# Low parts of split weights by an accumulating DMA instead of subtractions, in a two-layer decoder step

## The chip, the cores and the metric

The kernel runs on one core of a Trainium2 chip. The metric is the device time of one execution in microseconds (us), as the median over runs. A core has TensorE (PE: matmuls; its weight loads are listed apart as PEld), VectorE (DVE), ScalarE (ACT), GpSimd (POOL), SyncE (SP: here it issues most DMAs) and sixteen DMA engines that move data between HBM and the on-chip SBUF. Matmul results go to PSUM, which TensorE fills and VectorE and ScalarE empty.

## The reference

One inference step of two layers over 520 rows (512 prompt rows and 8 sample rows) of 1024 channels, in float32:

```
layer 0:  z = x @ w_in                     # 1024 -> 7 * 1024
          a_val, a_gate, b_post, c_pre, h, g = split(z)
          a = silu(layer_norm(causal_conv31(a_val * sigmoid(a_gate))))
          s = causal_conv3(c_pre * h)
          x = layer_norm(alpha * x + (concat(a, b_post * s) * silu(g)) @ w_out)
layer 1:  u, v, g = split(x @ w_in)        # 1024 -> 3 * 2048
          u, v = gelu(u), layer_norm(gelu(v))
          mix = tril(w_s) @ v + b          # in chunks of 128 rows, 8 heads
          x = layer_norm(alpha * x + (u * mix * silu(g)) @ w_out)
```

The step also returns the convolutions' new caches and the sample rows' v. Both convolutions run per channel.

## The kernel before

Channels lie on the 128 partitions and rows along the free axis, so that x is eight tiles of 128 x 520. All weights are cut into 136 *units* of 128 output channels by 1024 inputs ([128, 8, 128], 512 KB). The products keep float32 accuracy with TensorE's float32r type in three matmuls each: a weight unit is split into `hi` (its float32r rounding) and `lo` (what is left), x likewise, and a product is hi x hi + lo x hi + hi x lo. A unit over all 520 rows is 48 matmuls (8 k tiles, 2 halves of 260 rows, 3 terms) in `mm2` (L152, matmul at L157); `mm` does one half in 24 (L141).

Units 0 and 1 are loaded and split tile by tile together with x at the start (from L179, products at L207, tiles `w0h`, `w0l`). The 134 others come through `load_unit` (L116): SyncE loads `raw` (L119, three buffers), ScalarE casts it to `whi` (L121), and VectorE or GpSimd subtracts to get `wlo` (L124). GpSimd has the units of `ON_POOL`, 4 to 45 and 66 to 83, VectorE the other 74. `whi` and `wlo` take two of twelve slots, so six units are held; four units that are used while others are loaded take slots of their own. `unit(n)` (L132) calls `load_unit` up to `LEAD` = 5 units ahead of the product that asks for unit n.

The order of each engine's queue is fixed when the kernel is built: a scheduler simulates the program and places each instruction by its simulated time and priority. The taps of the wide convolution have the lowest priority and so fill what VectorE has left. At run time every queue is in order and waits for semaphores.

In layer 0 each i of eight needs four units: gate, value, c and h (z_gate, z_val, z_c, z_h). ScalarE takes the sigmoid `sg` of the gate (L291) and copies c (L317), VectorE makes `apad` (L306) and `ch` (L325), GpSimd copies the sample rows and sends the caches out (L307, L308, L326, L327). The wide convolution is 30 multiply-adds per tile on VectorE (L269) into `acc` in PSUM; the short one two (L332) into `sB` in SBUF, with `ch` in SBUF as well. Then z_post (VectorE multiplies it into `sB`, L392), the gates, and the two parts of the output projection with the layer norm (`out_part`: L487 to L562, its shift matmul at L497). The products `z` have two PSUM buffers; a third and a fourth, in which the products of unit 1 also lie, belong to the convolution. Layer 1 runs v in 16 units, scales it on VectorE (L658), and then takes u, gate and output in groups of four; `mix_unit` copies its sample rows on GpSimd (L725).

Of the kernel before, what the change touches and what calls it, by code (L numbers as in the profile page):

```python
# [9 lines left out]
F32 = mybir.dt.float32  # L10
# [3 lines left out]
ALU = mybir.AluOpType  # L14
# [3 lines left out]
D = 1024  # L18
# [14 lines left out]

# columns of the packed per-channel parameters
PA_W = 0
# [15 lines left out]
def decoder_kernel(  # L51
# [19 lines left out]
    nc = tc.nc  # L71
# [39 lines left out]

# [1 line left out]
    n_units = 2 + wu.shape[0]  # L113
    units = [None, None]

    def load_unit(wtag=("W", 12)):  # L116
        n = len(units)
        raw = wpool.tile([P, KT, P], F32, tag="raw", name=f"raw_{n}", bufs=3)
        nc.sync.dma_start(raw, wu[n - 2])  # L119
        hi = wpool.tile([P, KT, P], F32R, tag=wtag[0], name=f"whi_{n}", bufs=wtag[1])  # L120
        nc.scalar.copy(hi, raw)  # L121
        lo = wpool.tile([P, KT, P], F32R, tag=wtag[0], name=f"wlo_{n}", bufs=wtag[1])
        eng = nc.gpsimd if n in ON_POOL else nc.vector
        eng.tensor_tensor(lo, raw, hi.bitcast(F32), op=ALU.subtract)  # L124
        units.append((hi, lo))

    ON_POOL = set(range(4, 46)) | set(range(66, 84))
    EXTRA = set()
# [35 lines left out]

    # products of a constant until the first rows are there, so that the array's clock is up by then
    warm = const.tile([P, P], BF16, name="warm")
# [4 lines left out]

    # the input rows come with the first two weight units, one k tile after the other, and the
    # products follow in that order
    xh, xl = [], []
# [4 lines left out]
    for k in range(KT):  # L179
        x = tmp(f"x_{k}")  # L180
        if k % 4 == 0:
            raw = wpool.tile([P, 4, 2, P], F32, tag="raw", name=f"raw_s{k}", bufs=3)
# [4 lines left out]
        cuts = 2 if k == 0 else 1  # L187
# [29 lines left out]
    nc.sync.dma_start(pa, pa_in)  # L217
    # powers of two, so float32r holds them as well
    ones_r = const.tile([P, P], F32R, name="ones_r")
# [10 lines left out]

    # ================= layer 0 =================
    unit(1)
# [49 lines left out]
    n = 0  # L282
# [57 lines left out]

    # the sample rows of both convolutions
    nc.gpsimd.dma_start(cbs_out, xb)
# [27 lines left out]

    # layer norm of the wide convolution over the channels, then silu
    def mean_of(m, src, name):
        """the sum of src / D over the channels, from its two float32r parts"""
        both = tpool.tile([P, T], F32R, tag="B", name=f"parts_{name}", bufs=4)
        nn = src.shape[-1]
        hi, lo = both[:, :nn], both[:, TH : TH + nn]
        nc.scalar.copy(hi, src)
        nc.vector.tensor_tensor(lo, src, hi.bitcast(F32), op=ALU.subtract)
        nc.tensor.matmul(m, ones_r, hi, start=True, stop=False)
        nc.tensor.matmul(m, ones_r, lo, start=False, stop=True)  # L380
# [13 lines left out]
    def split_y(i, g, other, tag, parts):  # L394
        """y = g * other as its two parts, in that many cuts of the rows"""
        h = y_slot(F32R, f"yh_{tag}{i}")
        lo = y_slot(F32R, f"yl_{tag}{i}")
        for j in range(parts):
            c = slice(j * T // parts, (j + 1) * T // parts)
            nc.vector.tensor_tensor(g[:, c], g[:, c], other[:, c], op=ALU.mult)  # L400
            nc.scalar.copy(h[:, c], g[:, c])
            nc.vector.tensor_tensor(lo[:, c], g[:, c], h[:, c].bitcast(F32), op=ALU.subtract)
        yh.append(h)
        yl.append(lo)
# [68 lines left out]
    def out_part(base, c0, c1, yh, yl, res, lnc, done, last=False, pool_sub=()):  # L473
        """The second half of an output projection for the rows c0..c1, the residual, and the layer
        norm over the channels. The sums of the norm are of the rows less the mean of their first
        512 channels, so that no large mean cancels in the variance."""
        c = slice(c0, c1)
# [107 lines left out]

    # ================= layer 1 =================
    wt = wpool.tile([P, NH, P], F32, tag="M", name="wt", bufs=4)
    nc.gpsimd.dma_start(wt, wsT_in)
    bs = wpool.tile([P, NH, P], F32, tag="M", name="bs", bufs=4)
    nc.gpsimd.dma_start(bs, bs_in)  # L590
    # wt[s, h, t] is kept where s <= t
    nc.gpsimd.affine_select(
        wt, wt, pattern=[[0, NH], [1, P]], compare_op=ALU.is_ge, fill=0.0, base=0, channel_multiplier=-1
    )
    # and its float32r parts, for the column sums
    wth, wtl = [], []
# [31 lines left out]
    for i in range(NVF):  # L628
        z = one(i, f"z_v{i}_1")[:, :TH]
        mm(z, unit(n + i), x1h, x1l, hs(1))  # L630
        t = vt[i]
# [18 lines left out]
    def v_finish():  # L650
# [5 lines left out]
        for i in range(NV):  # L656
            for c in range(NC):
# [7 lines left out]
                )  # L665
        # column sums of the causal weights, for the shift of the norm
        for j in range(2):
# [5 lines left out]
            )  # L673
        # the sample rows' layer norm
        ssum = tiny.tile([P, NS], F32, name="ssum")
# [113 lines left out]
def _units(w, e0, e1):  # L789
    """[1024, e] columns e0..e1 as [n, 128 (k inside), 8 (k tile), 128]"""  # L790
    w = w[:, e0:e1]
    n = (e1 - e0) // P
    return w.reshape(KT, P, n, P).transpose(2, 1, 0, 3)


def _chan(a, n):
    """[..., n*128] -> [128, n, ...]"""
    a = a.reshape(a.shape[:-1] + (n, P))
    k = a.ndim
    return a.transpose((k - 1, k - 2) + tuple(range(k - 2)))  # L800
# [86 lines left out]
```

## Time and profile before

| | |
|---|---|
| time, median of 3 runs | 842.21 us (840.75 to 844.86) |
| profiled execution | span 840.8 us; its own time is not listed apart, the fastest run is 840.75 |
| granted TensorE clock, mean | 0.991 |
| busy, share of the span | PE 97%, DVE 66%, ACT 37%, POOL 23% |
| DMA | 82.38 MB, mean 98 GB/s; the sixteen engines' packets took 31.2% of the span |
| weight loads (L119) | 134 of 512 KB, median 3.6 us from issue to landing |

A row of the groups of instructions reads: line, engine, operation, out<-in, shapes, count | busy us, mean ns of one | idle time of its engine just before, and what ended it. A row of the stretches reads: from:to, its length, then busy us (and instructions) of PE, PEld, DVE, ACT and POOL, the granted clock of TensorE, the mean busy share of the DMA engines, and GB/s. A row of the timeline reads: start, us, engine, line, operation, count [idle before <- what ended it]. An engine that is not the bottleneck may idle at no cost.

### The profile page before, as it was taken

The page shows a single profiled execution, that of the slowest core. Times are in us where ns is not written, and L with a number is a line of the kernel's source. Part 1 is how long each engine was busy: PE and PEld are TensorE (multiplying, and loading weights), DVE is VectorE, ACT ScalarE, POOL GpSimd, SP SyncE. Part 2 cuts the span into 40 slices and gives each one's busy share as a digit, 9 for nine tenths or more (in the row PEclk, how much of TensorE's full clock was granted, in tenths as well). Part 3 has the DMA queues.
Part 4 walks back from the last instruction along what each step waited for, and adds up shares of the span by engine and source line. Part 5 has one row for each costly group of instructions (what it writes and reads, how often), then busy time and mean ns, then how long its engine had stood idle before and what let it go on. Part 6 is the DMA issues. An engine that isn't in the chain of part 4 may idle for free.

```text
span 840.8 us, 15982 instructions
## 1 busy us (share of the span) xinstructions
PE 816.4 (97%) x6792; PEld 813.8 (97%) x6792; DVE 557.8 (66%) x894; ACT 309.5 (37%) x470; POOL 193.7 (23%) x178
## 2 busy tenths in 40 slices
PE   9989999998999999999999999999999999999994
PEld 8989999998999999999999999999999999999993
DVE  5899999999994487356696333495455433625566
ACT  5423322333124346333466533333432133333243
POOL 0844355544340000024252711101000000000022
PEclk9999999999999999999999999999999999999998
DMA  8533333223223452424050522204223233222011
GB/s 301 164 103 101 101 103 102 96 82 130 72 79 101 122 166 66 126 76 126 26 166 12 171 81 82 95 24 156 77 76 95 82 101 94 83 79 99 1 51 51
DMA packets 27110, 82.38 MB, mean 98 GB/s; under 512 B 3568, under 2 KB 7296, under 8 KB 27040
## 3 DMA queue, kind: packets, MB, share of 16 engines
q1 hardware_dynamic: 26000, 79.01, 30.1%
q0 software_dynamic: 1040, 2.36, 0.7%
q8 instruction: 53, 0.87, 0.4%
q14 instruction: 17, 0.14, 0.1%
HBM read 77.91 MB, written 3.44 MB: 97 GB/s over the span
## 4 chain that ended last, share of the span: by engine, by line
PE 71%; DVE 23%; DMA 2%; issue 2%; ACT 1%; SPq 0%; POOL 0%; ACTq 0%; DVEq 0%; POOLq 0%
DVE acc L269 14%; PE z_gc L157 11%; PE z_u L157 11%; PE z_p L141 9%; PE z_v L157 7%; PE z_q L157 5%; PE z_o L157 5%; PE z_gb L157 5%; PE z_ga L157 5%; PE z_post L157 4%; PE z_v L141 4%; DVE sB L332 3%; DMA raw<-in_wu 2%; PE mix L713 2%; PE vt L615 1%
## 5 line engine op out<-in xcount | busy, mean ns | idle before, releaser
L121 ACT CAST whi<-raw 128x1024 fp32r<-128x1024 f32 x134 | 140.0, 1047 | 300.6 <-issue 66.6
L124 POOL TENSOR_TENSOR wlo<-raw,whi 128x1024 fp32r<-128x1024 f32 x60 | 145.6, 2434 | 262.6 <-ACT whi L121 262.3
L124 DVE TENSOR_TENSOR wlo<-raw,whi 128x1024 fp32r<-128x1024 f32 x74 | 90.2, 1222 | 131.0 <-ACT whi L121 131.0
L269 DVE SCALAR_TENSOR_TENSOR acc<-apad,pa,acc 128x512 f32<-128x512 f32 x240 | 166.6, 748 | 2.5 <-ACT acc L266 0.8
L157 PE MATMUL z_gc<-x1h,whi 128*128 128x260 f32 x256 | 72.9, 285 | 0.0
L157 PE MATMUL z_u<-x1h,whi 128*128 128x260 f32 x256 | 72.4, 283 | 0.0
L157 PE MATMUL z_gc<-x1h,wlo 128*128 128x260 f32 x256 | 72.0, 281 | 0.0
L157 PE MATMUL z_u<-x1l,whi 128*128 128x260 f32 x256 | 72.0, 281 | 0.0
L157 PE MATMUL z_gc<-x1l,whi 128*128 128x260 f32 x256 | 72.0, 281 | 0.0
L157 PE MATMUL z_u<-x1h,wlo 128*128 128x260 f32 x256 | 72.0, 281 | 0.0
L157 PEld LDWEIGHTS z_u<-x1h,wlo 128*128 128x128 f32 x256 | 48.1, 188 | 0.1
L157 PEld LDWEIGHTS z_gc<-x1h,wlo 128*128 128x128 f32 x256 | 48.2, 188 | 0.0
L157 PEld LDWEIGHTS z_u<-x1h,whi 128*128 128x128 f32 x256 | 48.1, 188 | 0.1
L157 PEld LDWEIGHTS z_gc<-x1l,whi 128*128 128x128 f32 x256 | 48.1, 188 | 0.0
L157 PEld LDWEIGHTS z_u<-x1l,whi 128*128 128x128 f32 x256 | 48.1, 188 | 0.0
L157 PEld LDWEIGHTS z_gc<-x1h,whi 128*128 128x128 f32 x256 | 48.1, 188 | 0.0
L725 POOL COPY mix<-mixs 128x8 f32<-128x8 f32 x16 | 3.5, 226 | 186.5 <-DVE gu L752 174.1
L157 PE MATMUL z_v<-x1h,whi 128*128 128x260 f32 x160 | 46.0, 287 | 0.0
L157 PE MATMUL z_v<-x1h,wlo 128*128 128x260 f32 x160 | 45.0, 281 | 0.0
L157 PE MATMUL z_v<-x1l,whi 128*128 128x260 f32 x160 | 44.9, 281 | 0.0
L157 PE MATMUL z_post<-xh,whi 128*128 128x260 f32 x128 | 36.8, 288 | 4.2 <-DVE sB L392 4.2
L157 PE MATMUL z_h<-xh,whi 128*128 128x260 f32 x128 | 36.9, 288 | 4.0 <-DVE apad L306 4.0
(259 smaller groups left out, 2758.5 us busy)
## 6 DMA issues: line engine op xcount, KB each, us to landing
raw<-in_wu SPq DMA_DIRECT2D x134, 512.0 KB, 3.6
xr<-in_xT SPq DMA_DIRECT2D x8, 260.0 KB, 4.6
x<-in_xT SPq DMA_DIRECT2D x7, 260.0 KB, 4.4
out_y<-r SPq DMA_DIRECT2D x8, 130.0 KB, 1.8
out_y<-out SPq DMA_DIRECT2D x4, 260.0 KB, 2.2
raw_s<-in_w SPq DMA_DIRECT2D x8, 128.0 KB, 4.2
xs<-in_cache_a SPq DMA_DIRECT2D x2, 496.0 KB, 9.2
out_cas<-xs POOLq DMA_DIRECT2D x2, 496.0 KB, 4.5
```

The lines of the kernel that those rows point to most:

```text
L121: nc.scalar.copy(hi, raw)
L124: eng.tensor_tensor(lo, raw, hi.bitcast(F32), op=ALU.subtract)
L141: nc.tensor.matmul(ps, a[:, k, :], b[k][:, c], start=(k == 0 and j == 0), stop=(k == KT - 1 and j == 2),)
L157: nc.tensor.matmul(z[h][:, :TH], a[:, k, :], b[k][:, hs(h)], start=(k == 0 and j == 0), stop=(k == KT - 1 and j == 2),)
L269: nc.vector.scalar_tensor_tensor(acc[i], apads[i][:, j : j + SEQ], pa[:, i, PA_W + j : PA_W + j + 1], acc[i], op0=ALU.mult, op1=ALU.add,)
L332: nc.vector.scalar_tensor_tensor(s[:, :SEQ], ch[:, j : j + SEQ], pa[:, i, PB_W + j : PB_W + j + 1], s[:, :SEQ], op0=ALU.mult, op1=ALU.add,)
L615: nc.tensor.transpose(m[:, c * P : (c + 1) * P], vt[i][:, c * P : (c + 1) * P], ident)
L713: nc.tensor.matmul(m[:, c * P : (c + 1) * P], vtok[i][:, c * P : (c + 1) * P], wt[:, h, :], start=True, stop=True)
L725: nc.gpsimd.tensor_copy(t[:, SEQ:], mixs[:, i, :])
```

## The change

Instead of subtracting, ScalarE writes the negated rounding of the unit, -hi, into `wlo` (L124), and a DMA issued on GpSimd reads the unit from HBM a second time and adds it onto `wlo` in SBUF (L125), which leaves w - hi. All 134 units of `load_unit` are done so; the table `ON_POOL` goes. Units 0 and 1, x and every other split stay as they were. (The diff also empties comments; these lines are left out.)

```diff
         hi = wpool.tile([P, KT, P], F32R, tag=wtag[0], name=f"whi_{n}", bufs=wtag[1])
         nc.scalar.copy(hi, raw)
         lo = wpool.tile([P, KT, P], F32R, tag=wtag[0], name=f"wlo_{n}", bufs=wtag[1])
-        eng = nc.gpsimd if n in ON_POOL else nc.vector
-        eng.tensor_tensor(lo, raw, hi.bitcast(F32), op=ALU.subtract)
+
+        nc.scalar.mul(lo, raw, -1.0)
+        nc.gpsimd.dma_start(lo, wu[n - 2], accum_op=ALU.add)
         units.append((hi, lo))
 
-    ON_POOL = set(range(4, 46)) | set(range(66, 84))
     EXTRA = set()
```

ScalarE's queue at the start, where units 2 and 3 (`whi_292` and its neighbour) are split while the first products still run, before:

```order
L200 CAST xh_272<-x_269 128x520
L121 CAST whi_292<-raw_290 128x1024
L121 CAST whi_313<-raw_311 128x1024
L291 ACT_TABLE_LOAD
L291 ACTIVATE sg_345<-z_first 128x520
L266 ACTIVATE acc_593<-apad_347,pa 128x512
```

and now:

```order
L200 CAST xh_272<-x_269 128x520
L121 CAST whi_292<-raw_290 128x1024
L124 ACTIVATE wlo_294<-raw_290 128x1024
L121 CAST whi_314<-raw_312 128x1024
L124 ACTIVATE wlo_316<-raw_312 128x1024
L291 ACT_TABLE_LOAD
L291 ACTIVATE sg_350<-z_first 128x520
L266 ACTIVATE acc_602<-apad_352,pa 128x512
```

Each cast is followed by the negation of the same unit, and two of these now stand ahead of the first sigmoid `sg`.

TensorE's queue where the first products (`z_first`) end and unit 2 is used for the first time (`z_c`), before:

```order
L207 MATMUL z_first_112<-xl_273,whi_s_205 128x260
L157 MATMUL z_c_354<-xh_120,whi_292 128x260
L157 MATMUL z_c_354<-xh_120,wlo_294 128x260
L157 MATMUL z_c_354<-xl_121,whi_292 128x260
L157 MATMUL z_c_354<-xh_120,whi_292 128x260
```

and now:

```order
L207 MATMUL z_first_112<-xl_273,whi_s_205 128x260
L157 MATMUL z_c_359<-xh_120,whi_292 128x260
L157 MATMUL z_h_417<-xh_120,whi_314 128x260
L157 MATMUL z_c_359<-xh_120,wlo_294 128x260
L157 MATMUL z_c_359<-xl_121,whi_292 128x260
```

One product of unit 3 (`z_h`), whose PSUM buffer is that of `z_first`, has come ahead of the first that uses unit 2's low part.

GpSimd's queue from the first convolution tile on, before:

```order
L307 COPY xs_335<-apad_347 128x8
L308 DMA out_cap<-apad_347 128x30
L124 TENSOR_TENSOR wlo_321<-raw_317,whi_319 128x1024
L124 TENSOR_TENSOR wlo_327<-raw_323,whi_325 128x1024
L124 TENSOR_TENSOR wlo_333<-raw_329,whi_331 128x1024
L124 TENSOR_TENSOR wlo_359<-raw_355,whi_357 128x1024
L326 COPY xb<-ch_466 128x8
L327 DMA out_cbp<-ch_466 128x2
```

and now:

```order
L125 DMA wlo_294<-in_wu 128x1024
L125 DMA wlo_316<-in_wu 128x1024
L307 COPY xs_340<-apad_352 128x8
L308 DMA out_cap<-apad_352 128x30
L125 DMA wlo_323<-in_wu 128x1024
L125 DMA wlo_330<-in_wu 128x1024
L125 DMA wlo_337<-in_wu 128x1024
L125 DMA wlo_364<-in_wu 128x1024
L125 DMA wlo_422<-in_wu 128x1024
L326 COPY xb<-ch_473 128x8
L327 DMA out_cbp<-ch_473 128x2
```

Every subtraction there has become the issue of a transfer, and units 2 and 3, which VectorE had, stand in this queue as well.

## The prediction

> **What bounds the kernel now.** The page's first part, then the waits of TensorE, then the groups of instructions.
>
> ```profile
> PE 816.4 (97%) x6792; PEld 813.8 (97%) x6792; DVE 557.8 (66%) x894; ACT 309.5 (37%) x470; POOL 193.7 (23%) x178
> ```
>
> TensorE is busy 816.4 of 840.8 us, so the 24 us around its matmuls are all that the change can win. Part of that is the start and the end of the program; the rest stands in the waits of TensorE (who waited for whom: us in total, times, longest).
>
> ```profile
> PE z_post L157 <- DVE sB L392: 4.2, 1, 4.2
> PE z_h L157 <- DVE apad L306: 4.0, 1, 4.0
> PE shift L497 <- DVE tot L492: 0.8, 1, 0.8
> PE z_c L157 <- DVE wlo L124: 0.2, 1, 0.2
> ```
>
> Two stalls of 4 us, both on VectorE. What made VectorE late before the one at 47 to 51 us is in the timelines of VectorE and GpSimd (start, us, instruction):
>
> ```profile
> 33.42 2.38 DVE L332 SCALAR_TENSOR_TENSOR sB<-ch,pa,sB 128x512 f32<-128x512 f32 x1 [0.91 <-ACT sB L330]
> 36.37 7.68 DVE L332 SCALAR_TENSOR_TENSOR sB<-ch,pa,sB 128x512 f32<-128x512 f32 x1
> 50.16 0.69 DVE L306 TENSOR_TENSOR apad<-z_val,sg 128x520 f32<-128x520 f32 x1
> ...
> 36.37 7.13 POOL L124 TENSOR_TENSOR wlo<-raw,whi 128x1024 fp32r<-128x1024 f32 x3
> ```
>
> One multiply-add of VectorE took 7.68 us and ended just after three subtractions of GpSimd that began with it (36.37 + 7.13 = 43.50). It reads two operands in SBUF. The wide convolution's steps, whose accumulator is in PSUM, never did this:
>
> ```profile
> L269 DVE SCALAR_TENSOR_TENSOR acc<-apad,pa,acc x240: 737/747/757, 23.4 to 247.5; 128x512 f32<-128x512 f32 x120
> L332 DVE SCALAR_TENSOR_TENSOR sB<-ch,pa,sB x16: 739/1154/7678, 33.4 to 207.1; 128x512 f32<-128x512 f32 x16
> L332 DVE SCALAR_TENSOR_TENSOR sB<-ch,pa,sB 128x512 f32<-128x512 f32 x16 | 29.3, 1831 | 0.9 <-ACT sB L330 0.9
> L358 DVE TENSOR_TENSOR proda<-xs,pa 128x992 f32<-128x992 f32 x2 | 6.5, 3273 | 0.0
> 160.00:200.00 40.00, 40.00 (x338) 40.00 (x338) 39.93 (x55) 11.31 (x15) 18.11 (x14) 1.00 0.32 106
> ```
>
> L332 runs in 739 ns alone and in 1831 ns on average: 16 x 1.09 = 17.5 us lost beside GpSimd. L358 (992 columns) should take about the 1.22 us of a VectorE subtraction of 1024 columns (L124 below): 2 x 2.05 = 4.1 us. So about 21 us of a VectorE that is full (39.93 of 40 us in the last row, third figure) go to waiting for GpSimd before 211 us.
>
> **The change part by part.** It removes the subtractions and adds a ScalarE pass and a second load per unit.
>
> ```profile
> L121 ACT CAST whi<-raw 128x1024 fp32r<-128x1024 f32 x134 | 140.0, 1047 | 300.6 <-issue 66.6
> L124 POOL TENSOR_TENSOR wlo<-raw,whi 128x1024 fp32r<-128x1024 f32 x60 | 145.6, 2434 | 262.6 <-ACT whi L121 262.3
> L124 DVE TENSOR_TENSOR wlo<-raw,whi 128x1024 fp32r<-128x1024 f32 x74 | 90.2, 1222 | 131.0 <-ACT whi L121 131.0
> L308 POOL DMA_DIRECT2D out_cap<-apad x8 | 4.7, 583 | 0.1
> ```
>
> Busy time: GpSimd loses 145.6 us and gains 134 issues of about 0.58 us (78 us); VectorE loses 90.2 us; ScalarE gains 134 x 1.05 = 140 us, to 450 of 841. None of these is on TensorE's path by itself. Behind each added ScalarE pass wait the evacuations of PSUM; two PSUM buffers give them one unit of TensorE's time, 5.7 us (row below), against 2.1 us for a cast and its negation: nothing, unless ScalarE is already late.
>
> *Won: the two stalls.* With no GpSimd arithmetic on weights VectorE is 21 us earlier by 211 us. It was 4.2 us too late there; closing the first stall brings TensorE's demands 5.6 us forward, and 21 covers both. After a stall the array is also slow for a while:
>
> ```profile
> 50.90:55.00 4.10, 4.09 (x21) 4.09 (x22) 4.07 (x7) 2.14 (x3) 4.06 (x4) 0.58 0.02 4
> 211.90:215.10 3.20, 3.12 (x15) 3.12 (x16) 3.20 (x4) 0.00 (x0) 1.82 (x1) 0.53 0.05 17
> 478.88 5.73 PE z_v L157 x48
> ```
>
> The granted clock was 0.58 and 0.53 in these stretches: 21 matmuls in 4.10 us where 5.73/48 = 0.119 us each gives 34, and 15 for 27: 1.6 and 1.4 us. Won: 4.0 + 1.6 + 4.2 + 1.4 = 11.2, and the 0.8 of the shift, where L561 was drawn out in the same way beside GpSimd. 12.0 us; bounds 12.0 and 0 (if VectorE's order and not GpSimd makes it late).
>
> *Lost: the start.* Unit 2, the first that comes through the changed code, is needed the moment the first products end:
>
> ```profile
> 17.71 0.28 PE L157 MATMUL z_c<-xh,whi 128*128 128x260 f32 x1
> 18.20 0.39 PE L157 MATMUL z_c<-xh,wlo 128*128 128x260 f32 x1 [0.20 <-DVE wlo L124]
> 15.84 1.05 ACT L121 CAST whi<-raw 128x1024 fp32r<-128x1024 f32 x1 [0.83 <-DMA raw<-in_wu]
> 18.80 1.05 ACT L121 CAST whi<-raw 128x1024 fp32r<-128x1024 f32 x1 [1.91 <-DMA raw<-in_wu]
> 19.86 1.28 ACT L291 ACT_TABLE_LOAD   x1
> 21.16 0.60 ACT L291 ACTIVATE sg<-z_first 128x520 f32<-128x520 f32 x1
> ```
>
> Its cast ends at 16.9, the negation at 17.95; only then does the accumulating transfer start, with the DMA engines full:
>
> ```profile
> 10.00:20.00 10.00, 9.80 (x82) 9.59 (x82) 5.95 (x11) 5.74 (x11) 0.00 (x0) 1.00 1.02 367
> raw<-in_wu SPq DMA_DIRECT2D x3, 512.0 KB, 5.9
> xs<-in_cache_a SPq DMA_DIRECT2D x2, 496.0 KB, 9.2
> out_cas<-xs POOLq DMA_DIRECT2D x2, 496.0 KB, 4.5
> ```
>
> No row shows an accumulating transfer. From 14 to 25 us a plain 512 KB took 5.9 us from issue to landing; an accumulate also reads its destination, one more pass of 0.524 MB / 367 GB/s = 1.43 us: 7.3 us, landing at 25.3, 7.1 us after 18.2. I take this value, since it is the row of the same size and place. From below: the new order puts a z_h product before the first low part, and that waits for the sigmoid to free its PSUM buffer, which ScalarE reaches at 18.80 + 2 x 1.05 + 1.28 + 0.60 = 22.8: 4.6 us at least. From above: 9.2 + 1.4 after 17.95 is 28.6, 10.4 us. With 1.5 us of slow clock: 8.6 us (6.1 to 11.9). The next units, one per 5.73 us, have their transfers issued by 21.5 and about 27 and are not late.
>
> The Trainium skill, "DMA: Bandwidth & Descriptors", section Anatomy of one DMA, fits 2.0 us plus bytes over 436 GB/s for a DMA issued on GpSimd, 3.2 us here; the row of 4.5 us above is already longer. By it the transfer lands near 21.2, the sigmoid decides, and the sum ends at its lower bound. That is a rival below.
>
> *Steady state.* A unit's slots come free five units, 28.7 us, before it is needed; casts 2.1, issue 0.6 and a landing even as at the start, 7.3, make 10. Hidden, if the DMA engines keep up: plain load 1.43 us of all sixteen engines, accumulate with two reads 2.86, together 4.29 of TensorE's 5.73 per unit. The bounds of the accumulate are 1.43 (the second read costs nothing) and no known top; the point where it decides is 4.30 us, three plain passes.
>
> In GpSimd's queue an accumulate now stands behind small copies that wait for others; the longest such waits are these:
>
> ```profile
> L612 POOL COPY vs<-v 128x8 f32<-128x8 f32 x16 | 8.5, 538 | 51.7 <-ACT v L641 51.7
> L725 POOL COPY mix<-mixs 128x8 f32<-128x8 f32 x16 | 3.5, 226 | 186.5 <-DVE gu L752 174.1
> ```
>
> Each waits for something that the program makes once per unit, so what is queued behind it (an accumulate, and TensorE five units later) loses at most one unit, 5.7 us: 15.7 of the 28.7. At the layers' boundary, where units are freed every 24 matmuls (2.9 us) instead of 48, eight units are freed before the first is used, and eight times 4.29 us of DMA fits into the 23 us of that pass plus the 17 of the next. Both cost nothing, and the full price of a lost cover would be a unit's stall, 5.7 + 1.5 us, at each place.
>
> One place eats most of the cover. VectorE scales v in one block of 16.5 us:
>
> ```profile
> 546.84 16.52 DVE L658 TENSOR_SCALAR vtok<-vtok,mv,rs 128x128 f32<-128x128 f32 x64 [0.41 <-POOL rs L655]
> ```
>
> If GpSimd cannot issue beside it, 16.5 + 10 = 26.5 of the 28.7 us are used; with a pile of two transfers behind it (2 x 2.86) 3.5 us are missing. I put 0 into the sum, since L308 was issued in 583 ns beside a VectorE that was full, and keep the case as rival D.
>
> The Trainium skill, "SBUF — State Buffer", section Two separate sides, speaks against the change here: a VectorE instruction in a two-port mode locks GpSimd out of the port through which it writes DMA descriptors. No GpSimd transfer runs beside L658 in this trace, so it shows neither.
>
> **Sum.** 840.8 - 12.0 + 8.6 = 837.4 us for the profiled execution. Its span is 840.8, the fastest run 840.75, the median 842.2, 1.4 above: 838.8 for the median, with the forecast's own range 836 to 842.
>
> **The rivals.**
> *A. The DMA engines become the bound (slower).* In the steady state, from 4.30 us per accumulate. For it: nothing here prices the addition, and the reads of weights double. Against: 4.29 of 5.73 with two reads. At three and a half passes a unit takes 6.44 us and 134 units 863; at four, 7.15 and 958. Each further pass adds 192 us.
> *B. The start is hidden further.* The landing is short and the sigmoid decides: 842.2 - 12.0 + 6.1 = 836.3. For it: POOL-issued transfers elsewhere took 4.5 us. Against: DMA share 1.02.
> *C. VectorE stays late.* The stalls come from the written order of its queue: 842.2 + 8.6 = 850.8. For it: VectorE is full even without the waiting. Against: 7.68 us beside 7.13.
> *D. The block of VectorE at 547 us holds GpSimd's transfers back.* 3.5 us missing and 1.5 of slow clock: 838.8 + 5.0 = 843.8. For it: the cover is down to 2.2 us there. Against: nothing like it beside the convolution.
>
> **How the numbers follow.** Forecast 0.48, B 0.22, A 0.18, C 0.07, D 0.05. A measurement of this kernel can tell about 0.5%, 4.2 us, from no change: faster is below 838.0, slower above 846.4. Of the forecast (836 to 842, centred on 838.8) a third is faster, 0.16, and 0.03 goes to a start that costs more than its bound, slower. Of B 0.20 is faster. Faster 0.16 + 0.20 = 0.36; slower A 0.18 + C 0.07 + 0.03 = 0.28; within 0.29 + 0.02 + D 0.05 = 0.36. The range reaches below to B with 2 us for stalls that I count as staying, 834, and above over C to where A begins, 858; what it leaves out is most of A, 0.17.
>
> **What would show it.** The waits of TensorE: no z_h on apad, no z_post on sB; a new one of z_c (or z_h) on the transfer or the sigmoid, 5 to 10 us, before 30 us. L332 back to 0.74 us each. DMA share near 0.75. Wrong, if TensorE waits for wlo all along (A), or if the two old stalls stand (C).

## The result and the profile after

The changed kernel takes 847.34 us in the median (846.28 to 848.2), the kernel before 842.21 (840.75 to 844.86): a ratio of 1.0055, with a 95% interval of 1.0039 to 1.0072. It is 0.55% slower where the forecast was 838.8 us, 0.4% faster. The profiled executions have spans of 845.0 and 840.8 us, so the 4.2 us can be followed in the traces, and what has to be explained is 845.0 against the 837.4 of the prediction's sum: 7.6 us.

The page of the changed kernel has these rows: the busy time of each engine with its share of the span, then the DMA queues with packets, MB and the share of the sixteen engines' span that their packets took. The software queue had 2.36 MB in the kernel before; the 134 accumulates bring it to 72.62.

```profile
PE 817.8 (97%) x6792; PEld 814.2 (96%) x6792; DVE 431.2 (51%) x820; ACT 433.6 (51%) x604; POOL 159.1 (19%) x252
...
q0 software_dynamic: 20336, 72.62, 46.3%
q1 hardware_dynamic: 26000, 79.01, 33.0%
```

VectorE is down by 126.6 us, GpSimd by 34.6, ScalarE up by 124.1, and the engines of the DMA are taken for 79% of the span, where the prediction had 75. All of this moved the way that was forecast, though GpSimd fell by only half as much as the 68 us of the prediction (145.6 less 78), since an accumulate took it 868 ns to issue and not 580. None of it is the time: TensorE's waits are (who waited for whom: us in total, times, longest).

```profile
PE z_c L157 <- DMA wlo<-in_wu: 4.7, 1, 4.7
PE z_h L157 <- ACT sg L291: 4.2, 1, 4.2
PE z_p L141 <- DMA wlo<-in_wu: 2.3, 1, 2.3
...
PE vt L615 <- ACT vtok L617: 0.9, 2, 0.6
PE z_p L141 <- ACT yh_a L401: 0.7, 1, 0.7
PE z_v L141 <- DMA wlo<-in_wu: 0.2, 1, 0.2
```

The old waits of z_h on apad, of z_post on sB and of the shift are gone. Two new ones stand at the start, and another, which was not forecast, in the output projection of layer 0 (z_p).

Where the 4.2 us lie is read from the first and the last matmul of each product. Such a row of the trace (one tile's instructions: durations in ns, then first and last start in us), for the changed kernel:

```profile
L157 PE MATMUL z_gate<-xh,whi x112: 277/282/286, 40.9 to 183.2; 128*128 128x260 f32 x112
L157 PE MATMUL z_post<-xh,whi x128: 277/282/286, 200.6 to 245.9; 128*128 128x260 f32 x128
```

and for the kernel before:

```profile
L157 PE MATMUL z_gate<-xh,whi x112: 277/282/387, 29.6 to 178.7; 128*128 128x260 f32 x112
L157 PE MATMUL z_post<-xh,whi x128: 277/282/584, 196.2 to 247.3; 128*128 128x260 f32 x128
```

z_gate begins 11.3 us later and z_post only 4.4 later: the start lost, the stage between won. Cut in this way, the span of every kernel of this study falls into the stages below, all from one profiled execution each. The start runs from the last matmul of z_first to the first of z_gate, and so on; the stage z_p runs to the first matmul of z_v, and z_v to that of z_u. "Ends" holds what lies before and after.

| us | start | z_gate to z_post | z_post to z_p | z_p | z_v | z_u to the last z_p | ends | span |
|---|---|---|---|---|---|---|---|---|
| before | 12.0 | 166.6 | 189.5 | 49.5 | 99.0 | 292.5 | 31.7 | 840.8 |
| after | 23.4 | 159.7 | 183.9 | 53.1 | 100.9 | 292.5 | 31.5 | 845.0 |
| difference | +11.4 | -6.9 | -5.6 | +3.6 | +1.9 | 0 | -0.2 | +4.2 |

So 12.5 us were won in the two stages with the old stalls, where the prediction had 11.2 for them: the other 0.8 of its 12.0, the wait of the shift, stood at 429 us and so in the stage z_p. There the kernel is 3.6 us slower in spite of that gain. In all 11.4 + 3.6 + 1.9 were lost, where the prediction had 8.6.

### The profile page after: what moved, and what is told of

Its sections match the earlier page's. It is cut to its first block, busy times and chain, and to the rows that moved or that the text cites. A ratio compares the mean times of both kernels' runs of the same rounds, so it can differ in the third digit from the quotient of the medians.

```text
span 845.0 us, 16147 instructions
## 1 busy us (share of the span) xinstructions
PE 817.8 (97%) x6792; PEld 814.2 (96%) x6792; DVE 431.2 (51%) x820; ACT 433.6 (51%) x604; POOL 159.1 (19%) x252
## 3 DMA queue, kind: packets, MB, share of 16 engines
q0 software_dynamic: 20336, 72.62, 46.3%
## 4 chain that ended last, share of the span: by engine, by line
PE 85%; DMA 6%; issue 4%; ACT 2%; DVE 1%; POOL 0%; SPq 0%; ACTq 0%; DVEq 0%; POOLq 0%
PE z_gc L157 11%; PE z_u L157 11%; PE z_v L157 6%; PE z_c L157 6%; PE z_p L141 5%; PE z_q L157 5%; PE z_o L157 5%; PE z_post L157 5%; PE z_gb L157 5%; PE z_h L157 5%; PE z_val L157 5%; PE z_gate L157 5%; PE z_ga L157 4%; DMA raw<-in_wu 3%; PE z_v L141 3%
## 5 line engine op out<-in xcount | busy, mean ns | idle before, releaser
L125 POOL DMA_DIRECT2D wlo<-in_wu x134 | 116.4, 868 | 543.2 <-ACT wlo L124 467.5
L269 DVE SCALAR_TENSOR_TENSOR acc<-apad,pa,acc 128x512 f32<-128x512 f32 x240 | 169.1, 751 | 5.1 <-ACT acc L266 2.5
L124 ACT ACTIVATE wlo<-raw 128x1024 fp32r<-128x1024 f32 x134 | 141.1, 1053 | 0.0
L157 PE MATMUL z_gc<-x1h,whi 128*128 128x260 f32 x256 | 72.9, 285 | 0.0
L157 PE MATMUL z_u<-x1h,whi 128*128 128x260 f32 x256 | 72.4, 283 | 0.0
L157 PE MATMUL z_u<-x1h,wlo 128*128 128x260 f32 x256 | 72.1, 282 | 0.0
L157 PE MATMUL z_gc<-x1h,wlo 128*128 128x260 f32 x256 | 72.0, 281 | 0.0
L157 PE MATMUL z_u<-x1l,whi 128*128 128x260 f32 x256 | 72.0, 281 | 0.0
L157 PE MATMUL z_gc<-x1l,whi 128*128 128x260 f32 x256 | 72.0, 281 | 0.0
L717 DVE SCALAR_TENSOR_TENSOR mix<-mix,pv,cm 128x512 f32<-128x512 f32 x16 | 12.0, 749 | 96.6 <-PE mix L713 96.6
L619 DVE BATCH_NORM_STATS2 stats<-vtok 128x6 f32<-128x128 f32 x64 | 13.9, 280 | 70.9 <-ACT vtok L617 70.9
L157 PEld LDWEIGHTS z_gc<-x1h,wlo 128*128 128x128 f32 x256 | 48.2, 188 | 0.0
L157 PEld LDWEIGHTS z_u<-x1l,whi 128*128 128x128 f32 x256 | 48.1, 188 | 0.0
L157 PEld LDWEIGHTS z_u<-x1h,wlo 128*128 128x128 f32 x256 | 48.1, 188 | 0.0
L157 PEld LDWEIGHTS z_u<-x1h,whi 128*128 128x128 f32 x256 | 48.0, 188 | 0.1
L157 PEld LDWEIGHTS z_gc<-x1l,whi 128*128 128x128 f32 x256 | 48.1, 188 | 0.0
L157 PEld LDWEIGHTS z_gc<-x1h,whi 128*128 128x128 f32 x256 | 48.1, 188 | 0.0
L157 PE MATMUL z_v<-x1h,whi 128*128 128x260 f32 x160 | 46.0, 288 | 0.0
L157 PE MATMUL z_v<-x1h,wlo 128*128 128x260 f32 x160 | 45.1, 282 | 0.0
L157 PE MATMUL z_v<-x1l,whi 128*128 128x260 f32 x160 | 45.0, 281 | 0.0
L157 PE MATMUL z_c<-xh,wlo 128*128 128x260 f32 x128 | 37.2, 291 | 4.7 <-DMA wlo<-in_wu 4.7
```

Of the source, the lines that this page charges most:

```text
L124: nc.scalar.mul(lo, raw, -1.0)
L125: nc.gpsimd.dma_start(lo, wu[n - 2], accum_op=ALU.add)
L157: nc.tensor.matmul(z[h][:, :TH], a[:, k, :], b[k][:, hs(h)], start=(k == 0 and j == 0), stop=(k == KT - 1 and j == 2),)
L269: nc.vector.scalar_tensor_tensor(acc[i], apads[i][:, j : j + SEQ], pa[:, i, PA_W + j : PA_W + j + 1], acc[i], op0=ALU.mult, op1=ALU.add,)
L619: nc.vector.bn_stats(stats[:, c, i, :], t[:, c * P : (c + 1) * P])
L717: nc.vector.scalar_tensor_tensor(t[:, :SEQ].rearrange("p (c t) -> p c t", c=NC), m.rearrange("p (c t) -> p c t", c=NC), pv[:, i, 0:1], cm[ ...
```

## The experiments

Line numbers shift by a few lines in the variants (`load_unit` grows), so that L157 can be L163 and L125 L129. Spans and stages are of one execution, medians of all runs of a kernel; the profiled execution lay up to 2.8 us from the median of its kernel, so differences of that size are read from the stages and waits and not from the totals.

### Undoing the start

The low parts of the first two units through the old subtraction, and in a second kernel those of the first six:

```diff
-        nc.scalar.mul(lo, raw, -1.0)
-        nc.gpsimd.dma_start(lo, wu[n - 2], accum_op=ALU.add)
+        if n in ON_DVE or n in ON_POOL:
+            eng = nc.gpsimd if n in ON_POOL else nc.vector
+            eng.tensor_tensor(lo, raw, hi.bitcast(F32), op=ALU.subtract)
+        else:
+            nc.scalar.mul(lo, raw, -1.0)
+            nc.gpsimd.dma_start(lo, wu[n - 2], accum_op=ALU.add)
...
+    ON_DVE = {2, 3}
+    ON_POOL = set()
```

> Units 2 and 3 are subtracted on VectorE again; the 132 others keep the accumulating transfer. Theory 1, the prediction's (only the landing of the first accumulate is uncovered, the next units are not late): the whole start term of the changed kernel, 11.3 us (z_gate begins at 40.9 instead of 29.6), goes: 847.3 - 11.3 = 836 us, z_gate near 29.6. Theory 2 (the transfers themselves are late until the DMA engines are no longer full, at 60 us): unit 4 is needed at 17.6 + 2 x 5.73 = 29.1, its transfer starts near 25 and takes the 10.2 us of the stretch from 30 to 60 us; a stall of about 6 us and 1.5 us of slow clock moves to unit 4: 847.3 - 11.3 + 7.5 = 843.5 us.

> Units 2 to 7 are subtracted on VectorE; the others keep the transfer. Unit 8 is needed at 17.6 + 6 x 5.73 = 52 us, its transfer can be issued before 35: covered by both theories, 847.3 - 11.3 = 836 us (theory 1: as the kernel with two units; theory 2: 7.5 us faster than it). Against both, theory 3: the six subtractions of 1.22 us make VectorE late for the first convolution tile again, up to the old 5.6 us: 841.6 us.

| us | start | z_gate to z_post | z_post to z_p | z_p | z_v | span | median | ratio to before (95%) |
|---|---|---|---|---|---|---|---|---|
| units 2, 3 subtracted | 11.9 | 164.6 | 183.7 | 51.4 | 101.1 | 836.5 | 840.53 | 0.9983 (0.9965 to 1.0000) |
| units 2 to 7 subtracted | 11.9 | 159.8 | 183.7 | 56.6 | 99.5 | 834.8 | 836.04 | 0.9919 (0.9899 to 0.9938) |

The start falls back to 11.9 us in both, so all of the 11.4 belongs to units 2 and 3. But with two units the next stage is 4.9 us longer than in the changed kernel. The timeline of TensorE in that kernel:

```profile
29.26 0.28 PE L163 MATMUL z_gate<-xh,whi 128*128 128x260 f32 x1
32.57 0.42 PE L163 MATMUL z_gate<-xh,wlo 128*128 128x260 f32 x1 [3.03 <-DMA wlo<-in_wu]
```

Unit 4 now is the first with a transfer, and it is 3.0 us late; the other 1.9 us go to slow matmuls after that wait. Theory 2 is right in kind (7.5 us were expected, 4.9 came): the units behind the first were on time in the changed kernel only because the stall before them had given them 11 us. With six units subtracted no wait is left there. Theory 3, that VectorE would be late for it, falls: 159.8.

### What the transfer costs by itself

```diff
-        nc.gpsimd.dma_start(lo, wu[n - 2], accum_op=ALU.add)
+        nc.gpsimd.dma_start(lo, wu[n - 2])
```

> The second transfer of each unit without its addition: it overwrites instead of adding, so the low part is the whole weight; the addition and the read of the destination are left out, all else stays. Theory 1 (the accumulate costs one more pass of all engines for reading its destination): the landing falls from 7.7 to the 5.7 us of the plain load, the software queue's share from 46 to about 25% of the engines, the engines are no longer full from 30 to 60 us; the first transfer lands some 2 us sooner: span 842 to 843 us, and 2 to 3 us less at the boundary: 839 to 841. Rival (a transfer issued on GpSimd is slow whatever it does): 7.7 us and 46% stay, 845 us.

It took 837.16 us (ratio 0.9932, 0.9907 to 0.9957), with a span of 835.6. The page of this kernel: queue, groups, and the DMA issues (KB, then median us from issue to landing).

```profile
q0 software_dynamic: 20336, 72.62, 24.3%
...
L125 POOL DMA_DIRECT2D wlo<-in_wu x134 | 71.1, 531 | 569.2 <-ACT wlo L124 504.0
...
raw<-in_wu SPq DMA_DIRECT2D x134, 512.0 KB, 3.7
wlo<-in_wu POOLq DMA_DIRECT2D x134, 512.0 KB, 4.7
```

The same rows of the changed kernel:

```profile
L125 POOL DMA_DIRECT2D wlo<-in_wu x134 | 116.4, 868 | 543.2 <-ACT wlo L124 467.5
...
raw<-in_wu SPq DMA_DIRECT2D x134, 512.0 KB, 5.7
wlo<-in_wu POOLq DMA_DIRECT2D x134, 512.0 KB, 7.7
```

The software queue's time falls from 46.3% of 845.0 us to 24.3% of 835.6, by 188 us or 1.40 us of all engines per unit: the addition costs as much as one more pass over the data, as the prediction's 1.43 had it. GpSimd issues the plain one in 531 ns and the accumulate in 868.

The start is the surprise: 21.7 us, only 1.7 less than with the addition. TensorE's two waits, of this kernel first and then of the changed one:

```profile
21.26 0.59 PE L157 MATMUL z_h<-xh,whi 128*128 128x260 f32 x1 [3.39 <-ACT sg L291]
25.14 0.59 PE L157 MATMUL z_c<-xh,wlo 128*128 128x260 f32 x1 [3.29 <-DMA wlo<-in_wu]
```

```profile
22.03 0.56 PE L157 MATMUL z_h<-xh,whi 128*128 128x260 f32 x1 [4.17 <-ACT sg L291]
27.31 0.58 PE L157 MATMUL z_c<-xh,wlo 128*128 128x260 f32 x1 [4.72 <-DMA wlo<-in_wu]
```

The first transfers were issued at 17.71 and 18.49 us (GpSimd's timelines), so that TensorE went on 7.4 and 8.8 us after the issue: the addition is 1.4 us of it, and the plain transfer, 4.7 us in the median, takes 7.4 here.

### What makes the start so long

```diff
-        nc.sync.dma_start(t, cache_a[:, 4 * j : 4 * j + 4])
         xs.append(t)
...
+        if i == 1:
+            for j in range(2):
+                nc.vector.tensor_copy(xs[j][:, 0, 0, 0:1], sg[:, 0:1])
+                nc.sync.dma_start(xs[j], cache_a[:, 4 * j : 4 * j + 4])
...
```

> The changed kernel with the two 496 KB cache loads xs taken out of the start: they are issued after the second sigmoid, and the sample rows of the first three tiles are copied in after that; all units from 2 on keep the transfer. At the start the engines are full (1.02 to 1.05 from 10 to 60 us), and even the transfer without addition took 7.4 us there against 4.7 elsewhere. Theory 1 (the landing of the first accumulate is queueing behind what was issued before it): 1.02 MB less, 2.8 us of all engines at 367 GB/s, so it lands near 24.4 and not 27.2, and z_gate begins at 38 instead of 40.9: span 842. Rival (the 8.7 us are the accumulate's own, as its fastest landing anywhere is 5.2 and its median 7.7): at most 1 us sooner, z_gate at 40 or later.

Start 22.9 us, z_gate from 40.2, span 843.5, median 844.9 (ratio 1.0025, 1.0004 to 1.0045). The transfer left at 18.28 and z_c went on at 27.17: 8.9 us, against 8.8 with the caches. The gain that theory 1 forecast did not come. But the test was a weak one, as a stretch of this kernel shows (busy us by engine, granted clock, DMA share, GB/s):

```profile
20.00:30.00 10.00, 3.41 (x14) 3.12 (x15) 4.46 (x7) 8.13 (x9) 3.18 (x4) 0.54 0.96 243
```

From 20 to 30 us the share went from 1.05 only to 0.96, since loads of units took the place of the caches. How much of the 8.8 us is queueing and how much the accumulate's own stays open.

```diff
-        nc.scalar.mul(lo, raw, -1.0)
+        if n < 4:
+            nc.vector.tensor_scalar_mul(lo, raw, -1.0)
+        else:
+            nc.scalar.mul(lo, raw, -1.0)
```

> The changed kernel with the negations of units 2 and 3 on VectorE and not on ScalarE; their transfers stay. The sigmoid comes 2.1 us sooner. Theory 1 (the end of the two waits at the start is set by the landing of the first accumulate alone, the wait for the sigmoid lies inside it): the first wait shortens by 2 us, the second grows by as much, z_gate begins at 40 to 41 us as before. Rival (the two waits add up, 4.2 + 4.7): z_gate begins 2 us sooner, near 38.8.

One run of 845.03 us, span 843.3; z_gate from 38.8, which is the rival's number, but by another way. VectorE negates as soon as the load is there, so the transfer left at 16.40 and not at 18.49, and z_c went on at 25.28, again 8.9 us after the issue. This fits theory 1's view that the landing sets the end, but does not show that the two waits don't add up, because transfer and sigmoid moved together.

### The boundary of the layers

The wait of z_p at 403 us has its origin 20 us earlier, in ScalarE's queue. Its order there in the changed kernel (unit numbers stand behind `whi_` and `wlo_`):

```
L124 ACTIVATE wlo_67_4393<-raw_67_4389 128x1024
L401 CAST yh_a5_4383<-silu_a5_4381 128x520
L121 CAST whi_70_4554<-raw_70_4552 128x1024
L124 ACTIVATE wlo_70_4556<-raw_70_4552 128x1024
L121 CAST whi_68_4454<-raw_68_4452 128x1024
L417 ACTIVATE silu_a6_4444<-z_ga6_4388 128x520
L124 ACTIVATE wlo_68_4456<-raw_68_4452 128x1024
...
L121 CAST whi_71_4589<-raw_71_4587 128x1024
...
L121 CAST whi_69_4521<-raw_69_4519 128x1024
```

Units 70 and 71 have slots of their own (`EXTRA`), free early, and the scheduler put 70 ahead of 68. Before the change 68 stood ahead of 70. The load of unit 70 needs the buffer of unit 67, which ScalarE's added pass gives free at 375.6 us, and the head of the queue waits until it has landed. The timelines of SyncE, ScalarE, GpSimd and TensorE:

```profile
375.66 0.33 SPq L119 DMA_DIRECT2D raw<-in_wu  x1
```

```profile
381.90 1.05 ACT L121 CAST whi<-raw 128x1024 fp32r<-128x1024 f32 x1 [5.76 <-DMA raw<-in_wu]
```

```profile
384.20 0.86 POOL L125 DMA_DIRECT2D wlo<-in_wu  x1 [7.41 <-ACT wlo L124]
...
392.57 0.86 POOL L125 DMA_DIRECT2D wlo<-in_wu  x1 [1.57 <-ACT yh_a L401]
```

```profile
403.14 0.39 PE L141 MATMUL z_p<-yh_a,wlo 128*128 128x260 f32 x1 [2.33 <-DMA wlo<-in_wu]
```

The accumulates of units 70, 68, 71 and 69 leave in this order within 8.4 us; the last one, which the sixth product of z_p needs, is there 10.6 us after its issue, beside full engines (share 1.00 from 385 to 402). Either the queue's order or the full engines could be the cause.

```diff
+    ON_DVE = {68, 69, 70, 71}
```

> Units 68 to 71, the last four of the first output projection, are subtracted on VectorE; the others keep the transfer, the start included. Theory 1: the 2.3 us wait of z_p at 403 us and its slow clock, 3.6 us together, come from the DMA engines, which are full from 385 to 402 us while eight units are wanted at 2.9 us each: four accumulates less (about 3 us of all engines each) take the stall away, 847.3 - 3.6 = 843.7 us, z_u begins 3.6 us earlier than in the changed kernel. Rival: ScalarE's queue, in which the cast of unit 70 stands ahead of that of unit 68 and waited until 381.9 for its load, is late whatever follows it; then a wait for unit 69 of about 2 us stays: 846.5 to 847.3 us.

z_p fell from 53.1 to 51.5 us, the span to 842.3, the median to 842.25 (ratio 0.9997, 0.9984 to 1.0011). No wait of z_p on wlo is left, and a wait of 1.9 us on yh_a stands in its place; ScalarE still waits for the load of unit 70:

```profile
382.72 2.00 ACT L121 CAST whi<-raw 128x1024 fp32r<-128x1024 f32 x2 [7.73 <-DMA raw<-in_wu]
...
386.81 0.62 ACT L407 CAST yh_a<-silu_a 128x520 fp32r<-128x520 f32 x1 [1.59 <-DVE silu_a L406]
```

Neither theory as written: the transfers' wait went, as theory 1 has it, and the queue's lateness, the rival, showed through the activation behind the cast. The times do not decide it. The median is below theory 1's 843.7, but the profiled execution (844.37 us) is the second slowest of twelve. And in the changed kernel and the five others of this study with the same code in that stage z_p takes from 51.4 to 56.6 us, so that 51.5 is not clear of them. To separate the two, units 70 and 71 were moved ahead in the order, with every transfer kept:

```diff
+            if len(units) == 52:
+                early[70], early[71] = load_unit(("M", 4), 70), load_unit(("M", 4), 71)
+            m = len(units)
+            units.append(early[m] if m in early else load_unit(("M", 4) if m in EXTRA else ("W", 12)))
```

> As the kernel with units 2 to 7 on VectorE, and units 70 and 71, which have slots of their own, are loaded and split ahead of unit 52 and not in their turn, so that their casts no longer stand ahead of those of units 68 and 69 in ScalarE's queue. Nothing is computed less, no transfer goes. Theory 1 (the boundary is lost in ScalarE's queue: the cast of unit 70 waits there for its load, behind it the casts and accumulates of 68 and 69 and the last silu): the z_p stage falls from 56.6 to the 49.5 us of before the change, span 834.8 - 7.1 = 827.7 us, no wait of z_p on yh_a or wlo over 1 us. Theory 2 (the DMA engines: six units are still wanted at 2.9 us each, and a plain load and an accumulate take about 4.6 us of them): the wait on yh_a goes, a wait on wlo of 2 to 3 us stays, span 831 to 832.5 us.

z_p took 47.3 us instead of 56.6, with no wait there at all and six accumulates still to be done: theory 1's stage came, and theory 2's wait on wlo did not. These accumulates now left one by one, 5.7 us apart, the last at 380.32 us, and from 385 to 402 us the share was 0.11 and not 1.00. The full engines at the boundary were thus in good part the work of the late queue, which let four accumulates go at once. The move also takes the traffic of two units out of this place; what that gave by itself is not shown. What was not expected is a new wait of 2.9 us in the stage before, which grew from 183.7 to 188.2 (span 830.5 for the 827.7 expected, median 835.28, ratio 0.9914, 0.9889 to 0.9939, not to be told from the 836.04 without the early units): at unit 52 ScalarE has the layer norm of the wide convolution to do, and the early casts wait for loads ahead of it.

```profile
266.22 1.05 ACT L122 CAST whi<-raw 128x1024 fp32r<-128x1024 f32 x1 [5.42 <-DMA raw<-in_wu]
```

```profile
PE st L389 <- ACT parts_col L387: 2.9, 1, 2.9
```

> As the kernel with units 70 and 71 early and units 2 to 7 on VectorE, with the two early units ahead of unit 60 instead of 52. There the early units cost 4.5 us in z_gb (ScalarE waited for their loads beside the layer norm of the wide convolution) and the z_p stage fell to 47.3. Theory: away from that layer norm the 4.5 us go and the 47.3 stay: span 826 us. Rival: with the engines at 0.9 two more units of 4.6 us make loads late wherever they stand: 829 to 831 us.

With `len(units) == 60` that stage is back at 183.8 and z_p stays at 47.3. The span is 829.1, 3 us over the expected 826, since z_u to the last z_p took 296.2 us here, with a wait of 1.4 on yh_c at the last output projection, which no other run had. The median is 829.65 us (ratio 0.9858, 0.9831 to 0.9884), 6.4 us under the kernel that differs in the order alone (5.1 by the two ratios to the kernel before).

The kernel without addition had the faulty order, too, and its z_p took 47.4: its loads land in 3.7 us, ScalarE waited a little over 3 us for unit 70, and nothing came late:

```profile
377.67 1.05 ACT L121 CAST whi<-raw 128x1024 fp32r<-128x1024 f32 x1 [3.19 <-DMA raw<-in_wu]
```

So the loss takes both, an order that puts a late load at a queue's head and transfers that are slow enough to make it matter: it went when the order was changed, and when the addition was left out.

### Bringing back GpSimd's arithmetic

```diff
         nc.gpsimd.dma_start(lo, wu[n - 2], accum_op=ALU.add)
+        if 4 <= n < 46:
+            nc.gpsimd.tensor_tensor(raw, raw, hi.bitcast(F32), op=ALU.subtract)
```

> The changed kernel, and GpSimd subtracts again for units 4 to 45, into the unit's load buffer, where nobody reads it, after it has issued the transfer. Theory 1, the prediction's (the two old stalls came from GpSimd's arithmetic beside VectorE's operations on SBUF): L332's multiply-add rises from 0.74 to over 1 us on average, the wait of z_post on sB returns, the stage from z_gate to z_post grows from 159.7 towards the 166.6 us of before: span 845.0 + 5 to 12 us. Rival (VectorE was late by the order of its queue, and the new order mended it): 0.74 us, no wait on sB, 845 us. The load buffers are held about 2.4 us longer, which costs at most one such wait early on.

871.09 us (ratio 1.0346, 1.0314 to 1.0379), span 868.3; z_gate to z_post 179.4 us and the stage behind it 188.1. Its waits and the short convolution's group:

```profile
PE z_h L159 <- DVE apad L308: 13.6, 5, 4.2
...
PE z_post L159 <- DVE sB L394: 2.4, 1, 2.4
```

```profile
L334 DVE SCALAR_TENSOR_TENSOR sB<-ch,pa,sB 128x512 f32<-128x512 f32 x16 | 48.4, 3022 | 0.9 <-ACT sB L332 0.9
```

In the changed kernel the same group reads:

```profile
L332 DVE SCALAR_TENSOR_TENSOR sB<-ch,pa,sB 128x512 f32<-128x512 f32 x16 | 11.9, 745 | 0.9 <-ACT sB L330 0.9
```

Both old waits return, and 36.5 us of VectorE with them. The prediction's mechanism for the gain is shown: between 30 and 250 us TensorE waits 16.0 us for VectorE's apad and sB and for no transfer. The size, 23.3 us of span, is over the 5 to 12 expected; why it is more than before the change is not shown.

### The transfer only where it wins

> The accumulating transfer for units 6 to 45 alone, in place of GpSimd's subtractions beside the wide convolution; units 2 to 5 on VectorE, all others as before the change (66 to 83 on GpSimd). If the terms add up: the 12.0 us of the prediction (12.7 as seen) are won and neither the start (11.3) nor the boundary and the v stage (5.5) are paid: 842.2 - 12.7 = 829.5 us. If VectorE's lateness comes from the order of its queue and not from GpSimd's arithmetic: 842 us. If VectorE needs the two subtractions more (units 4, 5: 2.4 us) at the first convolution tile: a stall of up to 2.4 us there, 832 us.

> The accumulating transfer for units 8 to 45 alone; units 2 to 7 on VectorE, the others as before the change (66 to 83 on GpSimd). The kernel with units 6 to 45 lost 2.1 us to a z_c that waited for the sigmoid near 46 us; the kernel with units 2 to 7 on VectorE had no wait there. If that wait belongs to the two transfers of units 6 and 7 in the full DMA engines: span 829.9 - 2.1 = 827.8 us, 15 us under the kernel before. If it belongs to the subtractions on VectorE: 830 us or more.

> The kernel with the transfer for units 8 to 45 alone, and units 70 and 71 loaded and split ahead of unit 60. If the order of the casts costs something even where the low parts are subtracted: the z_p stage falls from 49.3 to the 47.3 us of the kernel with early units, span 828.4 - 2.0 = 826.4. If the early units delay ScalarE in the z_o stage as they did in the z_gb stage (4.5 us), 829 to 831.

```diff
+    ON_DVE = set(range(2, 8)) | set(range(46, 66)) | set(range(84, 136))
+    ON_POOL = set(range(66, 84))
```

| us | start | z_gate to z_post | z_post to z_p | z_p | z_v | span | median | ratio to before (95%) |
|---|---|---|---|---|---|---|---|---|
| transfer for 6 to 45 | 12.0 | 161.8 | 183.7 | 49.3 | 99.6 | 829.9 | 833.36 | 0.9890 (0.9870 to 0.9909) |
| transfer for 8 to 45 | 12.2 | 159.8 | 183.8 | 49.3 | 100.2 | 828.4 | 830.40 | 0.9854 (0.9832 to 0.9876) |
| the same, 70 and 71 early | 11.8 | 159.8 | 183.9 | 48.5 | 100.2 | 827.6 | 829.84 | 0.9856 (0.9831 to 0.9881) |

The lines of code are the second kernel's; the first has 2 to 5 in place of 2 to 7. For the first a median of 829.5 us was expected, and 833.36 came. Its profiled execution was the fastest, with a span of 829.9 where the same sum gives 828.1 (840.8 less 12.7), and 2.0 us of that are the wait of z_c on the sigmoid at 42 us and the slow clock after it. They go with units 6 and 7: 828.4 for the 827.8 expected. In the spans the terms add up to within 2 us; the median of the first kernel is 3.9 us off. Of the 2.0 us that the order was to give, 0.8 show in the stage and nothing in the median. The last two kernels and the one above with the transfer from unit 8 on and the early units ahead of unit 60 all take about 830 us, 1.4 to 1.5% under the kernel before and 2% under the changed one, and can't be told apart.

## Why the prediction was wrong

*What bounds the kernel* was right: TensorE's waits and its slow clock moved the span, not the other engines' busy time.

*The two stalls* were right in mechanism and nearly in size: 11.2 us forecast, 12.5 in the two stages, L332 at 745 ns each, and the arithmetic of GpSimd brings the waits back. A wait of 0.6 us of z_gate on c, which the prediction did not count, went with them. Rival C falls.

*The steady state* was right on average. The addition costs 1.40 us per unit (1.43 forecast), the share is 0.79 (0.75), and rival A falls: from 60 to 385 us TensorE never waited (its busy time fills both stretches), and from z_u to the last z_p both kernels take 292.5 us.

```profile
60.00:240.00 180.00, 180.00 (x1516) 180.00 (x1515) 165.61 (x245) 83.20 (x110) 39.41 (x61) 1.00 0.89 191
240.00:385.00 145.00, 145.00 (x1220) 145.00 (x1219) 49.84 (x75) 82.91 (x110) 21.56 (x25) 1.00 0.87 195
```

*The start* was mis-sized: 8.6 us forecast, 11.4 measured, inside its bounds of 6.1 to 11.9. The step that failed is the landing, "7.3 us, landing at 25.3". It took the plain loads' 5.9 us as its base and added 1.43 for the second read. The second read is right (1.4); the base is not, because it comes from a kernel without the second transfers. Stretches from 18 to 28 us, of the kernel before and then of the changed one:

```profile
18.00:28.00 10.00, 9.80 (x82) 9.80 (x83) 6.59 (x10) 6.98 (x8) 4.46 (x4) 1.00 0.59 201
18.00:28.00 10.00, 1.24 (x4) 0.94 (x5) 5.00 (x8) 8.46 (x10) 3.80 (x6) 0.70 1.05 300
```

Where the engines' share was 0.59 it is now 1.05. The kernel without addition shows what this does to plain transfers from 14 to 25 us:

```profile
raw<-in_wu SPq DMA_DIRECT2D x4, 512.0 KB, 7.2
wlo<-in_wu POOLq DMA_DIRECT2D x3, 512.0 KB, 7.4
```

The loads of SyncE, 5.9 us before, take 7.2 there, about as long as the transfers of GpSimd: so it is not the issuing engine that makes the difference. That leaves the fuller engines as the likely cause; how much of it they make is not shown. The accumulate left at 18.49, not at 17.95, and TensorE went on 8.8 us later, at 27.31. The other part is the slow clock, put at 1.5 us from stalls of 4 us; after waits of 4.2 and 4.7 us with one matmul between them it cost about 2.5 (11.4 less 8.9 of waits). The changed kernel's stretch:

```profile
20.00:30.00 10.00, 3.24 (x13) 2.94 (x14) 6.89 (x11) 7.74 (x10) 3.31 (x5) 0.60 1.05 283
```

The Trainium skill, "TensorE: Matmul & The Clock Gate", Part 1, puts the time of slow matmuls after an idle window at about 3.4 us, give or take half a microsecond by the phase of a free-running window. This trace has slow matmuls from 27.3 to 32.3 us, and from 404.4 to 407.8 after the wait at the boundary: the 3.4 us of the second agree, the 5.0 of the first do not. Rival B falls with this term: its short landing never came at the start.

*"The next units are not late"* was wrong and hidden: with units 2 and 3 out of the way, unit 4 was 3.0 us late. The cost at the start is not that of the first accumulate alone.

*The boundary*, put at nothing, cost 3.6 us, and 4.4 against a forecast that had the shift's 0.8 as won there. Kernels without any wait in this stage take 47.3 to 47.4 us; the kernel before lost 2.2 us on that, the changed one 5.8. The step that failed is "eight units are freed before the first is used, and eight times 4.29 us of DMA fits". The slot of unit 69 comes free only when unit 63 has been used (384.5 us), as the first product of z_p begins, and the reckoning was of the engines alone; it looked at no queue. The order of ScalarE's queue had moved there, unit 70 ahead of 68, and it puts at the head of the queue a cast whose load must wait until the added pass has freed its buffer. "Nothing, unless ScalarE is already late" stood in the prediction; here ScalarE was late.

*z_v* took 1.9 us more in this execution, with waits of 1.1 on ScalarE's vtok and on wlo. It is not settled that the change makes this: over all kernels the stage lies between 98.9 and 101.1 us, at 98.9 in one with all transfers and at 100.2 in one with none there.

*Rival D*, the block of VectorE at 547 us, falls. It ran beside GpSimd's issues this time:

```profile
551.93 16.52 DVE L658 TENSOR_SCALAR vtok<-vtok,mv,rs 128x128 f32<-128x128 f32 x64 [0.57 <-POOL rs L655]
```

```profile
554.50 1.01 POOL L125 DMA_DIRECT2D wlo<-in_wu  x1 [2.61 <-ACT wlo L124]
```

This issue and two more beside the block took 1.01, 0.97 and 0.91 us instead of 0.86, and no unit came late. So the rule of the Trainium skill that the prediction weighed here ("SBUF — State Buffer", Two separate sides) can have cost at most 0.15 us per issue in this place; whether L658 runs in a two-port mode the trace does not show.

The sum, mended: 837.4 + 2.8 for the start - 1.3 for the larger gain + 4.4 for z_p + 1.9 for z_v - 0.2 at the ends = 845.0. The start alone would have left the forecast inside its range of 836 to 842 (838.8 + 2.8 = 841.6); the boundary, which had no term, and z_v took it out.

## What to carry to other kernels

A row of the kernel before prices a transfer with the traffic of the kernel before. Where the change adds traffic at that very place, count how full the engines will be there, and ask of every unit behind the first whether it is on time once the first is. Where the change adds work to an in-order queue, look there for the places where the scheduler has turned the order round, since a queue's head that waits for a late load holds back all that stands behind it. A change that wins in one stage and loses in two others need not be given up: made for 38 of 134 units alone, or for 128 with the order mended, it takes 830 us against 842 and 847.

## What the runs showed of the hardware

An accumulating transfer of 512 KB took GpSimd 868 ns to issue against 531 for a plain one of the same shape, landed in 7.7 us against 4.7 in the median (in kernels whose engines were taken for 79 and 56% of the span), and took the engines 1.40 us longer. The bytes that the profile counts do not show this: the queue reports 72.62 MB in both, at 46.3 and 24.3% of the span. With full engines the changed kernel therefore shows 244 GB/s, at a share of 1.00, where plain loads showed 367 at 1.02:

```profile
385.00:402.00 17.00, 14.97 (x118) 14.13 (x117) 5.85 (x13) 6.86 (x11) 2.66 (x4) 1.00 1.00 244
```
